# A two-block transformer kernel: first products ahead of a modulation step, and modulation columns summed off TensorE

## The chip, the cores and the metric

The kernel runs on one NeuronCore of a Trainium2 chip. Its time is the device time of one execution in microseconds (us). The engines are TensorE (PE, matrix products), VectorE (DVE), ScalarE (ACT), GpSimd (POOL) and SyncE (SP), which issues the DMAs. Each engine executes its instructions in the order in which the program issues them, and waits at semaphores for the others.

## The reference, cut to what matters

Two transformer-like blocks follow each other on a sequence of 512 rows and 1024 channels, in fp32. The change lies in the first block only.

```python
mod = split((silu(c) @ ada_w + ada_b), 6)          # six vectors of 1024
h  = modulate(rmsnorm(x,  norm1_g), mod[0], mod[1])  # h*(1+scale)+shift
hc = modulate(rmsnorm(ctx, norm1_g), mod_c[0], mod_c[1])
z  = h @ w_in                 # q, k, v, spatial gate u and v, conv a and gate
kvc = hc @ w_in[:, 512:1536]  # keys and values of the context
att = neighbourhood_attention(q, k, v, kc, vc, na_rpb)
y  = concat(att, spatial_gating(u, v), conformer_conv(a, gate)) @ w_out
x  = x + mod[2] * y
h2 = modulate(rmsnorm(x, norm2_g), mod[3], mod[4])
x  = x + mod[5] * conv_ffn(h2, w_up, conv_w, w_down)
x  = rmsnorm(x, final_norm_g)
# second block: stick-breaking attention, gated convolution, feed-forward (unchanged)
```

The matrix `ada_w` has 1024 rows (8 groups k of 128) and 6144 columns, here counted as 12 chunks of 512. Chunks 0 to 3 are the first shift and scale, for `c` and `c_ctx`; chunks 4 and 5 are mod[2], 6 and 7 are mod[3], 8 and 9 are mod[4], 10 and 11 are mod[5], the gate of the feed-forward.

## The kernel before, in words

Activations lie with channels on the 128 partitions and the 512 rows along the free axis. Every large fp32 product is made of three products of split operands: ACT writes the high part (`whi`, `h_hi`, L201, L167, L170), DVE or POOL subtracts it for the low part (`wlo`, `h_lo`, L209, L168, L171), and PE multiplies hi by hi, lo by hi and hi by lo (L160 to L162).

Weights come in units of 1 MB through SP's queue into three raw buffers. `ws.need(u)` makes the split of the units up to two ahead and issues the next load as soon as a raw buffer is free, which is when DVE has made its `wlo`. SP's queue holds at most eight transfers that have not landed.

The stages around the change, in order:

1. *Start.* PE multiplies junk (L487, L489) while inputs come. `first_rows(k)` sums the chunks 0 to 3 of step k as four column strips of a 128x256 tile, ACT copies the sum to `arow`, `first_mod(k)` (L530, its products L533) brings it into columns, `first_h(k)` makes the modulated `h[k]` and `first_split(k)` the split weights.
2. *First loop*, k = 0 to 7: `first_mm` (L562) multiplies 6 column tiles that accumulate over k; rows and modulation of step k+2 lie between its two halves. From k = 3 on `ada_fetch` (DMA L573) loads four 256 KB tiles of `ada_w` a call.
3. *Input projection*, weight unit by weight unit: p_u(0), p_u(1), p_q[0](0), p_q[0](1), p_q[1](0), p_q[1](1), each a tile of 24 products of 512 columns. Behind each of them stands an `ada_tick`. Then come v tiles 0 to 3, with a tick behind 1 and 3, the context's v tiles, the second half of v with two `gating` calls between, and the k projection with the attention.
4. *Modulation.* A round is four chunks over the eight k. `ada_step` multiplies the four tiles of one k (L481) into four strips of one PSUM tile; behind the last k ACT copies the tile to `arow` (L584). A tick first runs `ada_end` if a round is complete: four products (L591) bring the row into columns and DVE adds the bias (L594). Then it does two steps and fetches two. Round 0 is the chunks 4, 5, 8, 9 and round 1 the chunks 6, 7, 10, 11; the `ada_end` of round 1 stands behind tile 1 of the second v loop (L873).
5. *Work of the other engines there.* DVE makes 60 conv taps (L697, L699) that are dealt out between its other instructions at a rate per tile. `make_hc` (from L757) makes the context's `hc`: DVE `cs` (L761), ACT `hc` (L765), DVE the low part (L767), for three, two and three k: behind p_q[0](1), p_q[1](0) and p_q[1](1). ACT takes the spatial gate's weights `sgw` (L733, `sg_hi`) and the transposed `vgt` (L751) behind p_q[0](0).
6. *Feed-forward.* For each of 22 column tiles two up products; `evac_up` (L1224) makes the convolution and the gated product on ACT, DVE and POOL. The down projection adds `mod[40:48]` times its product to x.

What sets the order is the code itself: it issues each engine's instructions in a fixed order, `tick` deals out the taps, and the tiles' buffers come from pools of 80 slots and 8 PSUM banks.

Of the kernel before, what the change touches and what calls it, by code (L numbers as in the profile page):

```python
# [9 lines left out]
F32 = mybir.dt.float32  # L10
F32R = mybir.dt.float32r
AF = mybir.ActivationFunctionType
ALU = mybir.AluOpType
AX = mybir.AxisListType

P = 128
T = 512
D = 1024
KD = D // P
# [112 lines left out]
def program(ctx: ExitStack, tc: tile.TileContext, A, outT):  # L132
    nc = tc.nc
    V, S, G, PE = nc.vector, nc.scalar, nc.gpsimd, nc.tensor

    def pool(name, bufs, space=None, stack=ctx):
        kw = {"space": space} if space else {"reuse_waits": "tile"}
        return stack.enter_context(tc.tile_pool(name=name, bufs=bufs, **kw))

    ps = pool("ps", 8, bass.MemoryType.PSUM)  # L140
    cp = pool("const", 1)
# [5 lines left out]
    def bank(name="bank", cols=T):  # L147
        return ps.tile([P, cols], F32, tag="b", name=name, padded_shape=[P, T])

    def slot(dt=F32, name="slot", cols=T):  # L150
        t = sl.tile([P, T], dt, tag="s", name=name)
        return t if cols == T else t[:, :cols]
# [11 lines left out]
    def split(hi, lo, src, scale=None, eng=None):  # L164

        if scale is None:
            S.activation(hi, src, AF.Copy)  # L167
            (eng or V).tensor_sub(lo, src, hi)  # L168
        else:
            S.activation(hi, src, AF.Copy, scale=scale)  # L170
            V.scalar_tensor_tensor(lo, src, scale, hi, op0=ALU.mult, op1=ALU.subtract)  # L171
# [87 lines left out]
    def tile_gen(pj, m, acts, b, ts=slice(0, T), ks=None):  # L259

        for n, k in enumerate(ks or range(pj.nk)):
            mm3(b[:, ts], pj.part(m, k), [a[:, ts] for a in acts[k]], n == 0, n == pj.nk - 1)
            yield 3

    def tiles(pj, ms, acts, evac):

        for m in ms:
            b = bank()
            yield from tile_gen(pj, m, acts, b)

            ws.hi(ws.early(pj.at[m, pj.nk - 1][0] + 1))
            evac(m, b)
            ws.lo()
            tick()

    def run(gen):
        for _ in gen:
            pass
# [163 lines left out]
    for k in range(KD):  # L442
        t = slot(name="xs")
# [8 lines left out]
    def pc(name, i, n=1):  # L452
        a = PCOL[name][0]
        return par[:, a + i : a + i + n]

    ones = cp.tile([P, 1], F32, name="ones")
    G.memset(ones, 1.0)
    ident = cp.tile([P, P], F32, name="ident")
# [8 lines left out]
    sc = cp.tile([P, KD, 32], F32, name="sc")  # L467
# [2 lines left out]

    sel = cp.tile([P, 2], F32, name="sel")
    V.tensor_reduce(out=sel, in_=ident.rearrange("p (g j) -> p j g", g=4)[:, 0:2, :], op=ALU.add, axis=AX.X)
    pick = ident.rearrange("p (g j) -> p g j", g=4)[:, :, 0]

    mod = cp.tile([P, 48], F32, name="mod")
# [3 lines left out]
    def ada_matmul(out, g, kk, rhs, start, stop):  # L479

        PE.matmul(out[32 * g : 32 * g + 32, : rhs.shape[1]], sc[:, kk, :], rhs, start=start, stop=stop,  # L481
                  tile_position=(0, 32 * g), skip_group_check=True)
# [5 lines left out]
    def idle(k, n=T):  # L488
        PE.matmul(junk[:, :n], ident, xs[k][:, :n], start=True, stop=True)  # L489
# [40 lines left out]
    def first_mod(k):  # L530
        b, r = fb.pop(k)
        for t in range(2):
            PE.matmul(b[:, 256 + 2 * t : 258 + 2 * t], r[:, t * P : (t + 1) * P], sel, start=True, stop=True)  # L533
        a = PCOL["ada_b"][0] + k
        ab = par[:, a : a + KD + 1 : KD].unsqueeze(2).to_broadcast([P, 2, 2])
        V.tensor_add(mod2[:, k], b[:, 256:260].rearrange("p (t v) -> p t v", t=2), ab)
        V.scalar_tensor_tensor(gs[:, k, :], mod2[:, k, 1, :], 1.0, pc("norm1_g", k).to_broadcast([P, 2]),
                               op0=ALU.add, op1=ALU.mult)

    def first_split(k):  # L540
        wr = fw[k]
        hi = whi_p.tile([P, 1024], F32R, tag="whi", name="whi")[:, : NF * P]
        lo = wlo_p.tile([P, 1024], F32R, tag="wlo", name="wlo")[:, : NF * P]
        S.activation(hi, wr, AF.Copy)
        V.tensor_sub(lo, wr, hi)
        fw[k] = hi, lo

    def first_h(k, between=None):
        h[k] = pair("h")
        s_ = mod2[:, k, 0, 0:1]  # L550
        V.scalar_tensor_tensor(xs[k], xs[k], gs[:, k, 0:1], rxs, op0=ALU.mult, op1=ALU.mult)
        S.activation(h[k][0], xs[k], AF.Identity, bias=s_)
        if between:
            between()
        V.scalar_tensor_tensor(h[k][1], xs[k], s_, h[k][0], op0=ALU.add, op1=ALU.subtract)

    def first_mm(k, ms):
        hi, lo = fw[k]

        for w_, a, s0, s1 in ((hi, 0, True, False), (lo, 0, False, False), (hi, 1, False, True)):  # L560
            for m in ms:
                PE.matmul(first[m], w_[:, m * P : (m + 1) * P], h[k][a], start=s0 and k == 0, stop=s1 and k == KD - 1)  # L562


    ROUNDS = (4, 5, 8, 9), (6, 7, 10, 11)
    ada_live, ada_todo, ada_bank = [], [(r, kk) for r in range(2) for kk in range(KD)], {}

    def ada_fetch():
        if ada_todo:
            r, kk = ada_todo.pop(0)  # L570
            raw = [slot(name="ada") for _ in range(4)]
            for t, c in zip(raw, ROUNDS[r]):
                nc.sync.dma_start(t, A["ada_w"][kk * P : (kk + 1) * P, c * T : (c + 1) * T])  # L573
            ada_live.append((r, kk, raw))

    def ada_step():
        r, kk, raw = ada_live.pop(0)
        if kk == 0:
            ada_bank[r] = bank("adab")
        for g in range(4):  # L580
            ada_matmul(ada_bank[r], g, kk, raw[g], kk == 0, kk == KD - 1)
        if kk == KD - 1:
            t = slot(name="arow")
            S.activation(t, ada_bank[r], AF.Copy)  # L584
            ada_ends.append((r, t))

    def ada_end():
        r, t = ada_ends.pop(0)
        b = ada_bank.pop(r)
        for q in range(4):  # L590
            PE.matmul(b[:, 4 * q : 4 * q + 4], t[:, q * P : (q + 1) * P], pick, start=True, stop=True)  # L591
        for g in (0, 2):
            j = 4 * ROUNDS[r][g]
            V.tensor_add(mod[:, j : j + 8].rearrange("p (g q) -> p g q", q=4),  # L594
                         b[:, :16].rearrange("p (q g) -> p g q", g=4)[:, g : g + 2],
                         pc("ada_b", j, 8).rearrange("p (g q) -> p g q", q=4))

    ada_ends = []

    def ada_tick(n=2):  # L600

        if ada_ends:
            ada_end()
        for _ in range(min(n, len(ada_live))):
            ada_step()
            ada_fetch()
# [14 lines left out]
    rxs = slot(name="rxs")  # L621
    S.activation(rxs, rxb, AF.Copy)
    first_rows(1)
    idle(1)
    del junk
    first_mod(1)
    first_h(1)
    first_split(1)
    first += [bank(f"first{m}") for m in range(NF)]
    for k in range(KD):  # L630
        if k + 3 < KD:
            first_ada(k + 3)
            first_w(k + 3)
        elif k == 5:
            ws.load(0)
        if k >= 3:
            ada_fetch()
        first_mm(k, range(3))
        if k + 2 < KD:
            first_rows(k + 2)  # L640
            first_split(k + 2)
        first_mm(k, range(3, NF))
        if k + 2 < KD:
            first_mod(k + 2)
            first_h(k + 2)
        del fw[k]
    wr_.clear()
    ws.need(0)
    cs = []
    for q in range(4):  # L650
        t = slot(name="cs")
# [66 lines left out]
    first_out()  # L718
    conv_taps()
    lv.rate = LR[0]  # L720
    run(tiles(p_u, (0,), h, evac_u))
    ada_tick()
    cacc = slot(name="cacc", cols=CTX)
    S.activation(cacc, cs[0], AF.Square)
    for k in range(1, KD):
# [20 lines left out]
    for i in range(4):  # L746
        b = bank("vgT", cols=256)
# [31 lines left out]
    for i in range(4):  # L779
# [3 lines left out]
        t = slot(F32R, "vn")  # L783
# [83 lines left out]
    for i in range(4):  # L867
        if i == 3:
            take(kg, KD + 1)
        v_tile(p_v[1], 1, h, i, vt[i])  # L870
        if i in (0, 2):
            gating(i // 2)
        if i == 1:  # L873
            ada_end()
    for i in range(3):
        for q in range(2):
            G.tensor_scalar(vs[i][q][0:64, :], vt[i][q][64:128, :], 1.0, 0.0, op0=ALU.mult, op1=ALU.add)
# [15 lines left out]
    def place(n):  # L893

        return n // 8, n % 4, n // 4 % 2
# [139 lines left out]
    for n in range(NA + OUT + 2):  # L1035
        if n < NA:
            hp, blk, j = place(n)
            if n in QD:
                i = 1 + QD.index(n)
# [37 lines left out]
        for i, steps in PLAN.get(n, ()):  # L1077
            if len(begun) == i:
                b = bank()
# [144 lines left out]
    def evac_up(i, b):  # L1224
        t = gate.pop(i)
        S.activation(t, t, AF.Silu)
        V.tensor_mul(t, t, b)  # L1227
        act[i] = pair("act")
        split(*act[i], t, eng=G)

    def between():
        V.scalar_tensor_tensor(gs2, mod[:, 32:40], 1.0, pc("norm2_g", 0, 8), op0=ALU.add, op1=ALU.mult)
# [40 lines left out]
    g = values()  # L1273
# [142 lines left out]
    for n in range(32 + O2 + 2):  # L1416
# [17 lines left out]
        q = n - O2  # L1434
# [111 lines left out]
    out = outT.rearrange("(k p) n -> p k n", p=P)  # L1546
# [47 lines left out]
    g = half_gen(1)  # L1594
    take(g, 6)
    r = half_root(0)
# [10 lines left out]
    for j in range(4):  # L1607
# [4 lines left out]
        else:  # L1612
            t = bank("fr").rearrange("p (k n) -> p k n", k=2)
# [21 lines left out]
```

## Time and profile before

| what | value |
|---|---|
| time, median of 3 runs | 1387.94 us (1387.94 to 1388.05) |
| profiled execution, its own time | 1387.97 us |
| its span | 1386.1 us |
| mean granted clock of TensorE | 0.997 |
| busy: PE, DVE, ACT, POOL | 99%, 57%, 40%, 17% |
| DMA read, written | 147.67 MB, 2.10 MB |

The span runs from the first to the last instruction; the execution's own time lies around it. Busy PE is the time in which at least one product is under way. The ends of products are modelled, so a product's time is best read from the start of the next one: 24 products of 512 columns are 72 split products. A record on PE is a pass: an fp32 product shows as two.

### The profile page before, as it was taken

The numbers are of one execution on the slowest core, as the hardware profiler recorded it, in microseconds if no ns is written. First come the engines' busy times: TensorE is split into PE (matmuls) and PEld (weight loads), VectorE is DVE, ScalarE is ACT, GpSimd is POOL, SyncE is SP. The second block draws the span as 40 slices with busy tenths as digits, with TensorE's granted clock in tenths as the row PEclk, the third lists the DMA queues.
The fourth block names the chain that finished last, engine by engine and source line by source line (L and its number), as shares of the span: only waits on it lengthen the run. The fifth ranks groups of instructions, "written<-read, shape, count | busy, mean of one in ns | idle before, by whom it ended". The sixth has DMA issues, their size and how long they took to land.

```text
span 1386.1 us, 18751 instructions
## 1 busy us (share of the span) xinstructions
PE 1369.9 (99%) x7468; PEld 1151.0 (83%) x7468; DVE 783.8 (57%) x1158; ACT 559.4 (40%) x901; POOL 238.8 (17%) x254
## 2 busy tenths in 40 slices
PE   9999999999999999999999999999999999999997
PEld 5768999898888888888888888888897888888887
DVE  4579688465444443434458964635378866663223
ACT  4433258445333333323345543323455534343231
POOL 0022324101111110112034431000231111110100
PEclk9999999999999999999999999999999999999998
DMA  9992452323232222322373122233211332222221
GB/s 362 376 350 92 121 136 66 125 89 108 77 120 92 91 99 76 107 84 91 91 199 112 41 92 91 91 110 104 92 62 65 122 113 97 91 84 84 84 84 61
DMA packets 140887, 160.41 MB, mean 116 GB/s; under 512 B 5633, under 2 KB 117505, under 8 KB 140801
## 3 DMA queue, kind: packets, MB, share of 16 engines
q1 hardware_dynamic: 139360, 156.91, 34.4%
q10 hardware_dynamic: 1440, 2.31, 0.5%
q8 instruction: 58, 0.95, 0.3%
q14 instruction: 29, 0.23, 0.1%
HBM read 147.67 MB, written 2.10 MB: 108 GB/s over the span
## 4 chain that ended last, share of the span: by engine, by line
PE 91%; DVE 4%; ACT 1%; issue 1%; POOL 1%; DMA 0%; POOLq 0%; SPq 0%; DVEq 0%; ACTq 0%
PE bank L160 24%; PE bank L162 24%; PE bank L161 24%; PE first L562 3%; PE v L160 1%; PE v L162 1%; PE v L161 1%; PE adab L481 1%; PE s L904 1%; PE pt L932 1%; DVE wlo L209 1%; PE f L160 1%; PE o L160 1%; PE o L161 1%; PE o L162 1%
## 5 line engine op out<-in xcount | busy, mean ns | idle before, releaser
L209 DVE TENSOR_TENSOR wlo<-wraw,whi 128x1024 fp32r<-128x1024 f32 (+1 forms) x211 | 275.7, 1314 | 106.6 <-ACT whi L201 106.4
L162 PE MATMUL bank<-h_hi,wlo 128*128 128x512 f32 (+1 forms) x816 | 304.2, 373 | 1.7 <-DVE wlo L209 1.7
L161 PE MATMUL bank<-h_lo,whi 128*128 128x512 f32 (+1 forms) x816 | 305.5, 374 | 0.2
L160 PE MATMUL bank<-h_hi,whi 128*128 128x512 f32 (+1 forms) x816 | 304.9, 374 | 0.0
L201 ACT ACTIVATE whi<-wraw 128x1024 fp32r<-128x1024 f32 (+1 forms) x211 | 217.3, 1036 | 102.4 <-PE bank L161 89.5
L160 PEld LDWEIGHTS bank<-h_hi,whi 128*128 128x128 f32 x816 | 153.6, 188 | 30.1 <-PE adab L481 1.7
L162 PEld LDWEIGHTS bank<-h_hi,wlo 128*128 128x128 f32 x816 | 153.5, 188 | 29.6 <-DVE wlo L209 2.5
L161 PEld LDWEIGHTS bank<-h_lo,whi 128*128 128x128 f32 x816 | 153.5, 188 | 28.2 <-DVE h_lo L1501 0.3
L168 POOL TENSOR_TENSOR act_lo<-cv,act_hi 128x512 fp32r<-128x512 f32 x44 | 61.2, 1392 | 429.0 <-ACT act_hi L167 429.0
L160 PE MATMUL bank<-act_hi,whi 128*128 128x512 f32 x308 | 119.8, 389 | 0.0
L161 PE MATMUL bank<-act_lo,whi 128*128 128x512 f32 x308 | 119.8, 389 | 0.0
L162 PE MATMUL bank<-act_hi,wlo 128*128 128x512 f32 x308 | 119.8, 389 | 0.0
L160 PE MATMUL bank<-hb_hi,whi 128*128 128x512 f32 x288 | 116.0, 403 | 1.5 <-DVE wt_lo L1397 1.5
L162 PE MATMUL bank<-hb_hi,wlo 128*128 128x512 f32 x288 | 112.5, 391 | 0.0
L161 PE MATMUL bank<-hb_lo,whi 128*128 128x512 f32 x288 | 112.4, 390 | 0.0
L167 ACT ACTIVATE act_hi<-cv 128x512 fp32r<-128x512 f32 x44 | 27.8, 633 | 129.3 <-DVE cv L1227 73.0
L161 PEld LDWEIGHTS bank<-act_lo,whi 128*128 128x128 f32 x308 | 57.8, 188 | 12.1
L162 PEld LDWEIGHTS bank<-act_hi,wlo 128*128 128x128 f32 x308 | 57.8, 188 | 12.0
L160 PEld LDWEIGHTS bank<-act_hi,whi 128*128 128x128 f32 x308 | 57.8, 188 | 11.9
L160 PEld LDWEIGHTS bank<-hb_hi,whi 128*128 128x128 f32 x288 | 54.1, 188 | 11.5 <-DVE wt_lo L1397 1.7
L162 PEld LDWEIGHTS bank<-hb_hi,wlo 128*128 128x128 f32 x288 | 54.1, 188 | 11.5
L161 PEld LDWEIGHTS bank<-hb_lo,whi 128*128 128x128 f32 x288 | 54.2, 188 | 9.0
(386 smaller groups left out, 2425.7 us busy)
## 6 DMA issues: line engine op xcount, KB each, us to landing
wraw<-in_w_in SPq DMA_DIRECT2D x23, 1024.0 KB, 5.4
wraw<-in_ffn_w_up SPq DMA_DIRECT2D x22, 1024.0 KB, 4.9
wraw<-in_w_up SPq DMA_DIRECT2D x22, 1024.0 KB, 4.9
ada<-in_ada_w SPq DMA_DIRECT2D x64, 256.0 KB, 5.5
ada<-in_ada_first SPq DMA_DIRECT2D x32, 256.0 KB, 5.8
wraw<-in_w_out SPq DMA_DIRECT2D x8, 1024.0 KB, 4.8
wraw<-in_ffn_w_down SPq DMA_DIRECT2D x8, 1024.0 KB, 5.0
wraw<-in_w_down SPq DMA_DIRECT2D x8, 1024.0 KB, 5.1
```

The costliest lines, as they stand in the source:

```text
L160: PE.matmul(out, lhs[0], rhs[0], start=start, stop=False, **kw)
L161: PE.matmul(out, lhs[0], rhs[1], start=False, stop=False, **kw)
L162: PE.matmul(out, lhs[1], rhs[0], start=False, stop=stop, **kw)
L167: S.activation(hi, src, AF.Copy)
L168: (eng or V).tensor_sub(lo, src, hi)
L201: S.activation(h, src, AF.Copy)
L209: V.tensor_sub(l, src, h)
L481: PE.matmul(out[32 * g : 32 * g + 32, : rhs.shape[1]], sc[:, kk, :], rhs, start=start, stop=stop, tile_position=(0, 32 * g), skip_group_ch ...
L562: PE.matmul(first[m], w_[:, m * P : (m + 1) * P], h[k][a], start=s0 and k == 0, stop=s1 and k == KD - 1)
L904: PE.matmul(st_s[n][:, ks], qp[hp][a][j][:, qs], k_, start=a == 0, stop=a == 1)
L932: PE.transpose(pt[:, c * P : (c + 1) * P], e[:, c * P : (c + 1) * P], ident)
```

## The change

It does four things.

1. The junk product `idle(1)` goes, and modulation, h and weight split of step 1 stand behind the first three column tiles of step 0.
2. Round 0: the steps k = 0, 1, 2 are not multiplied on PE. `ada_sum` in the first loop (k = 4, 5, 6) forms the sum over k for each of 128 partitions: four DVE products, four DVE multiply-adds, then four ACT products and four POOL additions. Four products with `one0` add the sum to the PSUM tile behind the last step.
3. Round 1 holds only chunks 6 and 7, two k per step, so four steps. The tick behind p_u(0) becomes three fetches ahead of it. The `ada_end` of round 1 has no place of its own any more: the next tick runs it.
4. Chunks 10 and 11 are fetched in the first eight up tiles of the feed-forward, two tiles at a time, summed over k on DVE in the next, and brought into columns by eight products of one column in tile 10.

```diff
+    ROUNDS = ([[(k, c) for c in (4, 5, 8, 9)] for k in range(KD)],
+              [[(2 * k + i, c) for i in range(2) for c in (6, 7)] for k in range(KD // 2)])
+    NV = 3
+    def ada_sum():
+        r, kk, raw = ada_live.pop(0)
+        for g in range(4):
+            if kk == 0:
+                ada_acc.append(slot(name="adaacc"))
+                V.tensor_scalar(ada_acc[g], raw[g], sc[:, kk, 0:1], 0.0, op0=ALU.mult, op1=ALU.add)
+            elif kk == NV - 1:
+                S.activation(raw[g], raw[g], AF.Copy, scale=sc[:, kk, 0:1])
+                G.tensor_add(ada_acc[g], ada_acc[g], raw[g])
+            else:
+                V.scalar_tensor_tensor(ada_acc[g], raw[g], sc[:, kk, 0:1], ada_acc[g], op0=ALU.mult, op1=ALU.add)
...
     def ada_step():
         r, kk, raw = ada_live.pop(0)
-        if kk == 0:
+        first_ = NV if r == 0 else 0
+        if kk == first_:
             ada_bank[r] = bank("adab")
         for g in range(4):
-            ada_matmul(ada_bank[r], g, kk, raw[g], kk == 0, kk == KD - 1)
-        if kk == KD - 1:
+            ada_matmul(ada_bank[r], g, ROUNDS[r][kk][g][0], raw[g], kk == first_, r == 1 and kk == KD // 2 - 1)
+        if r == 0 and kk == KD - 1:
+            for g in range(4):
+                PE.matmul(ada_bank[r][32 * g : 32 * g + 32, :], one0, ada_acc[g], start=False, stop=True,
+                          tile_position=(0, 32 * g), skip_group_check=True)
+        if kk == len(ROUNDS[r]) - 1:
             t = slot(name="arow")
             S.activation(t, ada_bank[r], AF.Copy)
...
+    def gate_fetch(k):
+        gate_raw.append([slot(name="ada") for _ in range(2)])
+        for i, t in enumerate(gate_raw[-1]):
+            ada_load(t, k, 10 + i)
+    def gate_step(k):
+        for i, t in enumerate(gate_raw.pop(0)):
+            if k == 0:
+                gate_acc.append(slot(name="gacc"))
+                V.tensor_scalar(gate_acc[i], t, sc[:, k, 0:1], 0.0, op0=ALU.mult, op1=ALU.add)
+            else:
+                V.scalar_tensor_tensor(gate_acc[i], t, sc[:, k, 0:1], gate_acc[i], op0=ALU.mult, op1=ALU.add)
+    def gate_end():
+        b = bank("gsum", cols=8)
+        for j in range(8):
+            PE.matmul(b[:, j : j + 1], gate_acc[j // 4][:, j % 4 * P : j % 4 * P + P], ones, start=True, stop=True)
+        V.tensor_add(mod[:, 40:48], b, pc("ada_b", 40, 8))
...
     first_rows(1)
-    idle(1)
     del junk
-    first_mod(1)
-    first_h(1)
-    first_split(1)
...
         first_mm(k, range(3))
+        if k == 0:
+            first_mod(1)
+            first_h(1)
+            first_split(1)
...
             first_h(k + 2)
+        if k in (4, 5, 6):
+            ada_sum()
...
+    for _ in range(3):
+        ada_fetch()
     run(tiles(p_u, (0,), h, evac_u))
-    ada_tick()
...
         if i in (0, 2):
             gating(i // 2)
-        if i == 1:
-            ada_end()
...
+        if 1 <= i < KD + 1:
+            gate_step(i - 1)
+        if i < KD:
+            gate_fetch(i)
+        if i == KD + 2:
+            gate_end()
```

What stands in PE's row of instructions behind v tile 1, in the kernel before (each row is one form, with the number of times that it stands there in a row; the last products of v tile 1 and the first of v tile 2 frame it):

```order
L161 MATMUL v<-wlo,h_hi 128x256
L162 MATMUL v<-whi,h_lo 128x256
L481 MATMUL adab<-ada,sc 32x512 x8
L160 MATMUL v<-whi,h_hi 128x256
L161 MATMUL v<-wlo,h_hi 128x256
```

The same place in the changed kernel:

```order
L161 MATMUL v<-wlo,h_hi 128x256
L162 MATMUL v<-whi,h_lo 128x256
L624 MATMUL adab<-pick_112,arow 128x2 x4
L160 MATMUL v<-whi,h_hi 128x256
L161 MATMUL v<-wlo,h_hi 128x256
```

The two steps of round 1 are gone from here, and its `ada_end`, which reads `arow`, stands in their place.

On ACT, from the last weight split and q tile to the copy `arow` of round 1, in the kernel before (`hc` is the context stream of the last `make_hc`, `v_hi` and `vn` are the high parts of the v tiles and of the normalised gate rows):

```order
L170 ACTIVATE q_hi<-bank 128x512
L765 ACTIVATE hc<-cs,mod_113 128x256 x3
L201 ACTIVATE whi<-wraw 128x1024
L167 ACTIVATE v_hi<-v 128x256
L167 ACTIVATE vn<-vgt 128x256
L167 ACTIVATE v_hi<-v 128x256
L167 ACTIVATE vn<-vgt 128x256
L167 ACTIVATE v_hi<-v 128x256
L167 ACTIVATE vn<-vgt 128x256
L167 ACTIVATE v_hi<-v 128x256
L167 ACTIVATE vn<-vgt 128x256
L584 ACTIVATE arow<-adab 128x512
```

The same place in the changed kernel:

```order
L170 ACTIVATE q_hi<-bank 128x512
L823 ACTIVATE hc<-cs,mod_115 128x256 x3
L615 ACTIVATE arow<-adab 128x512
L201 ACTIVATE whi<-wraw 128x1024
L167 ACTIVATE v_hi<-v 128x256
L167 ACTIVATE vn<-vgt 128x256
```

The copy has moved ahead of the four v tiles, and now stands directly behind the last three `hc`.

On SP, from the weight loads at the end of the first loop to the load of `sgw`, in the kernel before (`cs` is the context, `rows` are rows of the spatial gate):

```order
L185 DMA wraw<-in_w_in 128x8x256 x3
L652 DMA cs<-in_ctxT 128x2x256 x4
L573 DMA ada<-in_ada_w 128x512 x8
L185 DMA wraw<-in_w_in 128x8x256
L573 DMA ada<-in_ada_w 128x512 x8
L731 DMA rows<-in_rows 128x512
L732 DMA rows<-in_rows 128x256
L733 DMA sgw<-in_sg_wT 128x512
```

The same place in the changed kernel:

```order
L185 DMA wraw<-in_w_in 128x8x256 x3
L709 DMA cs<-in_ctxT 128x2x256 x4
L592 DMA ada<-in_ada_w 128x512 x12
L185 DMA wraw<-in_w_in 128x8x256
L592 DMA ada<-in_ada_w 128x512 x8
L789 DMA rows<-in_rows 128x512
L790 DMA rows<-in_rows 128x256
L791 DMA sgw<-in_sg_wT 128x512
```

Twelve modulation tiles instead of eight stand ahead of the next weight load, so four more ahead of `sgw`.

## Rows read from the trace of the kernel before

**Rows 1.** The page: busy us by engine, and the chain's shares by engine.

```profile
PE 1369.9 (99%) x7468; PEld 1151.0 (83%) x7468; DVE 783.8 (57%) x1158; ACT 559.4 (40%) x901; POOL 238.8 (17%) x254
...
PE 91%; DVE 4%; ACT 1%; issue 1%; POOL 1%; DMA 0%; POOLq 0%; SPq 0%; DVEq 0%; ACTq 0%
```

**Rows 2.** Windows: length, busy of PE, PEld, DVE, ACT, POOL, clock, DMA share, GB/s.

```profile
60.00:80.00 20.00, 20.00 (x103) 13.71 (x102) 12.48 (x13) 10.64 (x19) 7.61 (x7) 1.00 1.04 378
...
100.00:120.00 20.00, 20.00 (x146) 14.44 (x139) 18.77 (x31) 5.38 (x11) 9.38 (x12) 1.00 0.44 158
...
1378.00:1380.00 2.00, 0.31 (x3) 0.12 (x2) 1.65 (x3) 0.00 (x0) 0.82 (x1) 0.75 0.00 0
```

**Rows 3.** Timeline of PE: start, us, line, operation, tiles, records, idle before.

```profile
82.18 0.50 PE L391 MATMUL sums<-ones,cacc 128*128 128x1 f32 x4
...
115.04 1.92 PE L481 MATMUL adab<-ada,sc 128*32 128x512 f32 x16
116.90 0.39 PE L160 MATMUL v<-whi,h_hi 128*128 128x256 f32 x1
...
134.74 0.28 PE L162 MATMUL mix<-sg_hi,vn 128*128 128x256 f32 x1
...
137.74 0.95 PE L591 MATMUL adab<-ident,arow 128*128 128x4 f32 x8
138.55 0.36 PE L160 MATMUL v<-whi,h_hi 128*128 128x256 f32 x1
...
142.95 0.40 PE L160 MATMUL k<-h_hi,whi 128*128 128x512 f32 x1
```

**Rows 4.** Timeline of ACT, 84 to 126 us.

```profile
84.40 0.61 ACT L167 ACTIVATE sg_hi<-sgw 128x512 fp32r<-128x512 f32 x1
...
86.03 1.07 ACT L201 ACTIVATE whi<-wraw 128x1024 fp32r<-128x1024 f32 x1
91.07 0.60 ACT L170 ACTIVATE q_hi<-bank 128x512 fp32r<-128x512 f32 x1 [3.97 <-PE bank L162]
...
119.49 1.31 ACT L765 ACTIVATE hc<-cs,mod 128x256 fp32r<-128x256 f32 x3 [6.06 <-DVE cs L761]
...
124.90 0.60 ACT L584 ACTIVATE arow<-adab 128x512 f32<-128x512 f32 x1 [0.85 <-PE adab L481]
```

**Rows 5.** Timeline of DVE, 56 to 132 us.

```profile
56.40 2.36 DVE L209 TENSOR_TENSOR wlo<-wraw,whi 128x1024 fp32r<-128x1024 f32 x2 [0.20 <-ACT whi L201]
...
91.70 0.69 DVE L171 SCALAR_TENSOR_TENSOR q_lo<-bank,q_hi 128x512 fp32r<-128x512 f32 x1 [0.38 <-ACT q_hi L170]
...
105.54 4.63 DVE L699 SCALAR_TENSOR_TENSOR cacc<-ag,par,cacc 128x510 f32<-128x510 f32 x4
...
118.97 1.27 DVE L761 SCALAR_TENSOR_TENSOR cs<-cs,gs,rcbs 128x256 f32<-128x256 f32 x3
...
131.40 0.42 DVE L168 TENSOR_TENSOR vn<-vgt,vn 128x256 fp32r<-128x256 f32 x1
```

**Rows 6.** Timelines of ACT and PE at the start.

```profile
16.49 0.72 ACT L552 ACTIVATE h_hi<-xs,mod 128x512 fp32r<-128x512 f32 x1 [1.86 <-DVE xs L551]
...
18.02 0.61 PE L533 MATMUL ada<-sel,arow 128*128 128x2 f32 x4
18.49 0.94 PE L562 MATMUL first<-h_hi,whi 128*128 128x512 f32 x3
```

**Rows 7.** Timeline of SP's DMA issues: the load of sgw.

```profile
77.54 0.33 SPq L733 DMA_DIRECT2D sgw<-in_sg_wT  x1
```

**Rows 8.** DMA issues, 50 to 100 us: count, KB each, median us to landing.

```profile
sgw<-in_sg_wT SPq DMA_DIRECT2D x1, 256.0 KB, 4.8
```

**Rows 9.** PE's groups by form, 4.5 to 6.8 and 7.5 to 11 us: busy, mean ns.

```profile
L489 PE MATMUL junk<-xs,ident 128*128 128x512 f32 x2 | 1.9, 1061 | 0.0
...
L489 PE MATMUL junk<-xs,ident 128*128 128x512 f32 x7 | 3.4, 607 | 0.1
```

**Rows 10.** Timeline of DVE in the up tiles of the feed-forward.

```profile
410.88 0.75 DVE L1220 SCALAR_TENSOR_TENSOR cv<-bank,par,cv 128x511 f32<-128x511 f32 x1 [2.14 <-ACT cv L1218]
```

More of the change, by code (lines that the diff above doesn't have):

```diff
@@ L472, in program @@
     V.tensor_reduce(out=sel, in_=ident.rearrange("p (g j) -> p j g", g=4)[:, 0:2, :], op=ALU.add, axis=AX.X)
+    pick2 = cp.tile([P, 2], F32, name="pick2")
+    V.tensor_reduce(out=pick2, in_=ident.rearrange("p (i c j) -> p c i j", i=2, c=2)[:, :, :, 0], op=ALU.add, axis=AX.X)
     pick = ident.rearrange("p (g j) -> p g j", g=4)[:, :, 0]
@@ L562, in first_mm, with ada_load @@
                 PE.matmul(first[m], w_[:, m * P : (m + 1) * P], h[k][a], start=s0 and k == 0, stop=s1 and k == KD - 1)
-    ROUNDS = (4, 5, 8, 9), (6, 7, 10, 11)
-    ada_live, ada_todo, ada_bank = [], [(r, kk) for r in range(2) for kk in range(KD)], {}
+    ROUNDS = ([[(k, c) for c in (4, 5, 8, 9)] for k in range(KD)],
+              [[(2 * k + i, c) for i in range(2) for c in (6, 7)] for k in range(KD // 2)])
+    NV = 3
+    ada_acc = []
+    one0 = cp.tile([P, 32], F32, name="one0")
+    G.memset(one0, 0.0)
+    G.memset(one0[:, 0:1], 1.0)
+    def ada_sum():
[9 more added lines that the diff above has]
+                V.scalar_tensor_tensor(ada_acc[g], raw[g], sc[:, kk, 0:1], ada_acc[g], op0=ALU.mult, op1=ALU.add)
+    ada_live, ada_todo, ada_bank = [], [(r, kk) for r in range(2) for kk in range(len(ROUNDS[r]))], {}
+    def ada_load(t, k, c):
+        nc.sync.dma_start(t, A["ada_w"][k * P : (k + 1) * P, c * T : (c + 1) * T])
     def ada_fetch():
@@ L571, in ada_fetch @@
             raw = [slot(name="ada") for _ in range(4)]
-            for t, c in zip(raw, ROUNDS[r]):
-                nc.sync.dma_start(t, A["ada_w"][kk * P : (kk + 1) * P, c * T : (c + 1) * T])
+            for t, (k, c) in zip(raw, ROUNDS[r][kk]):
+                ada_load(t, k, c)
             ada_live.append((r, kk, raw))
@@ L589, in ada_end @@
         b = ada_bank.pop(r)
+        w_ = pick if r == 0 else pick2
+        n = w_.shape[1]
         for q in range(4):
-            PE.matmul(b[:, 4 * q : 4 * q + 4], t[:, q * P : (q + 1) * P], pick, start=True, stop=True)
-        for g in (0, 2):
-            j = 4 * ROUNDS[r][g]
+            PE.matmul(b[:, n * q : n * q + n], t[:, q * P : (q + 1) * P], w_, start=True, stop=True)
+        for g, j in ((0, 16), (2, 32)) if r == 0 else ((0, 24),):
             V.tensor_add(mod[:, j : j + 8].rearrange("p (g q) -> p g q", q=4),
-                         b[:, :16].rearrange("p (q g) -> p g q", g=4)[:, g : g + 2],
+                         b[:, : 4 * n].rearrange("p (q g) -> p g q", g=n)[:, g : g + 2],
                          pc("ada_b", j, 8).rearrange("p (g q) -> p g q", q=4))
+    gate_raw, gate_acc = [], []
+    def gate_fetch(k):
[14 more added lines that the diff above has]
+        V.tensor_add(mod[:, 40:48], b, pc("ada_b", 40, 8))
+        gate_acc.clear()
     ada_ends = []
```

## Prediction

> **What bounds the kernel now.** I read the page's busy times first, then its chain, then the stretches from 60 to 160 us engine by engine. TensorE (PE) is busy for 99% of the span and makes 91% of the chain that ended last [rows 1]. So PE work that disappears is time gained, unless PE comes to wait for something else. VectorE (DVE) is at 57% over the whole span, but that mean hides one stretch: from 100 to 120 us DVE is busy for 18.77 of 20 us [rows 2], and there its work, the conv taps and the context stream hc, runs behind PE. In the kernel before nobody on PE waits for the end of that backlog before the k projection. The reader is to hold on to this: PE is full everywhere, but from 83 to 148 us DVE and the ScalarE (ACT) work behind it are the late ones.
>
> **The change part by part.** The sum is made against the profiled execution, 1387.97 us (span 1386.1 and 1.87 around it), which is 0.03 above the median of 1387.94.
>
> *PE work removed.* A modulation tick of two steps is 16 records, from 115.04 to 116.90: 1.86 us; one step is 0.93 [rows 3]. An ada_end runs from 137.74 to 138.55: 0.81. In program order: the tick behind p_u(0) goes (−1.86, and about 0.2 for two changes of matmul shape: −2.06); the tick behind p_q[0](1) gains four one0 products, priced as a step (+0.93); the tick behind p_q[1](1) loses a step (−0.93); the tick behind v tile 1 becomes an ada_end (−1.86 + 0.81 = −1.05); the tick behind v tile 3 goes (−1.86); the ada_end in the p_v[1] loop goes (−0.81). Sum −5.8.
>
> *The place that decides: the ada_end that now stands between v tiles 1 and 2.* Its first product needs the copy arow of round 1. In the kernel before the copy is made at 124.90 [rows 4] and first read at 137.74 [rows 3], 12 us later. In the changed program the copy is issued on ACT behind the three hc of the last make_hc, and these wait for DVE's cs products. In the trace those cs start at 118.97 [rows 5], the first hc at 119.49 after ACT has been idle for 6.06 us waiting for them, and the three hc take 1.31 [rows 4]. With a copy of 0.60 the arow is there at 119.49 + 1.31 + 0.60 = 121.40, less S, by which DVE's chain moves forward. PE arrives far earlier: v tile 1 ends at 115.04, and what is removed ahead of it (0.8 at the start, below, 2.06, and +0.93 − 0.93) brings it there at 112.2. PE executes in order, so v tile 2 and all behind it wait 121.40 − 112.2 − S = 9.2 − S. Everything that was gained ahead of it is given back: from there on only the time of the copy counts.
>
> *How large S is.* DVE's chain from 83 us on starts with PE's q tiles, so at best S = 2.06 + 0.8 = 2.86. What may hold it: DVE's q_lo at 91.70 stood only 0.38 idle, behind ACT's q_hi at 91.07 [rows 4, 5], and ACT reaches q_hi through sg_hi, which waits for the transfer sgw. *The start*, for the 0.8: the first product follows h_hi(0), which ends at 17.21, instead of starting at 18.49, 1.28 earlier; the modulation pair that moves behind it costs its 0.47 (18.02 to 18.49) there: 0.8 [rows 6]. sgw is issued at 77.54 [rows 7] and lands 4.8 us later [rows 8], at 82.34; ACT took it at 84.40. Two things make it later. Four more ada transfers stand ahead of it on SP's queue: at 378 GB/s of a full DMA (share 1.04 [rows 2]) 262,144 bytes take 0.69 us, so 2.8. And the third weight load is issued when DVE has made the wlo of 56.40 to 58.76 [rows 5]; directly ahead of these now stand four scalar_tensor_tensor of ada_sum, 0.75 each by the row of that form [rows 10], 3.0 in all, of which the 0.8 of the start and the 0.2 idle there cover 1.0: +2.0. sgw lands at 87.1, and from sg_hi to the end of whi ACT takes 2.7 (84.40 to 87.10 [rows 4]): q_hi at 89.8, S = 1.3. The ends: no delay at the load leaves S at 2.86, since q_hi then waits for PE alone at 88.2; and if ada_sum's four POOL adds stretch the wlo beside them as POOL stretched the taps at 105.54 (four in 4.63, 1.16 each against 0.75 [rows 5, 10]), the two wlo take 1.3 more and S is 0.0. I take 1.3, worked out from the nearest rows. The Trainium skill ("GPSIMD Engine Reference", 8. Key points) says that GpSimd shares its SBUF interfaces with VectorE and collides with DVE instructions of two SBUF inputs; the 1.16 agrees, and by that rule alone S would be the 0.0.
>
> *From the copy to the k projection.* In the trace 27.91 us pass from 115.04 to 142.95 [rows 3]; of these 1.86, 1.86 and 0.81 go and 0.81 for the moved ada_end come in: 24.2. So k starts at 121.40 − 1.3 + 24.2 = 144.3 against 142.95: +1.35. Nothing between waits longer than that: DVE and ACT work of the v tiles moves with PE's stall.
>
> *The clock.* With S = 1.3 PE stands still for 7.9 us. The trace shows both levels: the first junk matmuls of 128x512 take 1061 ns a record and the later ones 607 [rows 9], so PE, which began at 1.46, ran at the 1.2 GHz level until about 6.8; and at the end, when PE's work runs out (busy 0.31 in 1378 to 1380), the granted clock of that slice is 0.75, a fall from 1.00 to 0.50 in the middle of it [rows 2]. Nowhere in the trace does PE pause for 8 us and go on. If it falls here, the nearest row for the price is the start: 5.3 us at the lower level, in which 1 − 607/1061 = 43% is lost: 2.3 us. Bounds 0 (no fall) and 2.7 (half of 5.3). I take 2.3, since the end shows a fall sooner than 8 us after the last long group. The Trainium skill ("TensorE: Matmul & The Clock Gate", Part 1) says the same from the other side: the throttled 1.2 GHz is the default, and only activity lifts it. By this rule the loss comes; without a fall the sum is 2.3 less.
>
> *The feed-forward gate.* gate_end adds 8 products of one column, 16 records. By L391 (four in 0.50 [rows 3]) they are 2.0, by the ada_end (eight in 0.81) 1.6; I take 1.8, on PE between two up tiles and covered by nothing: +1.8. The 16 DVE products (two per up tile, 0.75 each, 1.5) fall into DVE's waits for PE, 2.14 idle in the tightest of the rows that I read there [rows 10]; the 16 transfers stand behind a weight load each. Cost nothing, and 12 us if that cover were gone.
>
> *Sum.* +1.35 (all before k) + 2.3 (clock) + 1.8 (gate) = +5.4: 1387.97 + 5.4 = 1393.4. From the bounds: S 2.86 and no fall give −0.2 + 0 + 1.6 = +1.4 (1389.4); S 0.0, 2.7 and 2.0 give +2.65 + 4.7 = +7.4 (1395.3).
>
> **The rivals.** (a) *PE waits, but the clock stays.* For it: no row shows a pause of this length inside the work, so the fall is not proven. Against: the fall at the end. Time: 1393.4 − 2.3 = 1391.1.
> (b) *The copy is in time and the change pays, faster than before.* One point decides: the arow copy ends by 112.2, so S would have to be 9.2. For it: the taps that fill DVE are not urgent, and ACT is idle for 6.06 there. Against: DVE's own order puts cs behind them, and its 18.77 of 20 us. Then PE keeps −5.8 − 0.8; next late is vn, whose last low half ends at 131.82 [rows 5] and is read at 134.74 [rows 3], 2.9 later; PE would come there 2.86 + 1.05 + 1.86 = 5.8 earlier and DVE 1.3, so it waits 1.6. Sum −6.6 + 1.6 + 1.8 = −3.2: 1384.8.
> (c) *The gate's DVE work is not hidden.* For it: each up tile already has DVE's two conv products, a product and the weight split. Against: 2.14 of idle for 1.5. In full 12 us: 1405. It decides if DVE has no idle left in up tiles 1 to 8.
>
> **How the numbers follow.** This kernel's measurement can tell 0.2%, 2.8 us, from no change: 1385.2 to 1390.7. Forecast, with a fall: 0.60; (a) 0.18; (b) 0.13; (c) 0.09. The forecast case spans 1391.5 to 1395.3; (a) 1389.4 to 1393, half of it within the bound; (b) lies faster but for a little; (c) slower. Faster 0.12, same 0.12, slower 0.76. The range takes in the forecast, (a) and the lower part of (c), and leaves (b) and a full (c) out: 1388.5 to 1396.5.
>
> **What would show it.** Right: on PE an idle time of 6 to 9 us ahead of the pick2 products, released by ACT's arow; hc's ACT idle before them, released by DVE's cs; sgw landing about 5 us later than before and q_hi released by ACT, not by PE; a granted clock of 0.50 for some us behind the stall; k at 143 to 146; gsum 1.6 to 2.0 with no new DVE wait of PE in the up tiles. Wrong: no idle at the pick2 products (then b), a clock of 1.00 throughout (a), or up tiles longer than before (c). The step I am least sure of is S, the one that I am surest of the order on ACT.

## The result and the profile after

The changed kernel takes 1400.0 us (1399.47 to 1400.54, 4 runs) against 1387.99 for the kernel before: ratio on record 1.0083, interval 1.0071 to 1.0096 (not quite the quotient of the two medians). It is 12.0 us slower; the forecast was 5.4 slower, with a range that ended at 1396.5. The profiled execution is 1399.72, its span 1398.0 against 1386.1, so 11.9 of the difference lie in the span.

Where PE waited, in the changed kernel (us in total, times, longest):

```profile
PE adab L624 <- ACT arow L615: 10.9, 1, 10.9
PE bank L162 <- DVE wlo L209: 2.7, 4, 1.0
PE bank L160 <- DVE wt_lo L1459: 1.5, 1, 1.5
...
PE bank L160 <- ACT vgt L809: 0.6, 1, 0.6
```

In the kernel before the first and the last of these do not exist, and the second is shorter:

```profile
PE bank L162 <- DVE wlo L209: 1.7, 3, 0.8
```

So there is one large new wait, and it stands between v tiles 1 and 2. The timeline of PE there, and at the start of the k projection, answers to [rows 3]:

```profile
113.94 0.28 PE L162 MATMUL v<-whi,h_lo 128*128 128x256 f32 x1
125.14 1.87 PE L624 MATMUL adab<-pick,arow 128*128 128x2 f32 x8 [10.92 <-ACT arow L615]
126.87 0.56 PE L160 MATMUL v<-whi,h_hi 128*128 128x256 f32 x1
...
151.90 0.40 PE L160 MATMUL k<-h_hi,whi 128*128 128x512 f32 x1
```

PE came at 114.2 and went on at 125.1. The ada_end took 1.73 us to the next start, where one of its length took 0.81 before, and k starts at 151.90 instead of 142.95. What PE waited for, on ACT (answers to [rows 4]):

```profile
92.28 0.63 ACT L167 ACTIVATE sg_hi<-sgw 128x512 fp32r<-128x512 f32 x1 [9.39 <-DMA sgw<-in_sg_wT]
...
94.82 0.62 ACT L170 ACTIVATE q_hi<-bank 128x512 fp32r<-128x512 f32 x1
...
123.30 1.30 ACT L823 ACTIVATE hc<-cs,mod 128x256 fp32r<-128x256 f32 x3 [6.06 <-DVE cs L819]
124.51 0.57 ACT L615 ACTIVATE arow<-adab 128x512 f32<-128x512 f32 x1
```

ACT stood 9.39 us idle for sgw; q_hi came at 94.82 instead of 91.07, and everything that DVE does behind q_lo came as much later: hc at 123.30 instead of 119.49. Read upwards, DVE and POOL show why sgw was late (answers to [rows 5]):

```profile
55.31 4.82 DVE L587 SCALAR_TENSOR_TENSOR adaacc<-ada,sc,adaacc 128x512 f32<-128x512 f32 x4
60.05 5.67 DVE L209 TENSOR_TENSOR wlo<-wraw,whi 128x1024 fp32r<-128x1024 f32 x3
...
95.46 0.69 DVE L171 SCALAR_TENSOR_TENSOR q_lo<-bank,q_hi 128x512 fp32r<-128x512 f32 x1 [6.87 <-ACT q_hi L170]
```

```profile
56.21 7.29 POOL L585 TENSOR_TENSOR adaacc<-adaacc,ada 128x512 f32<-128x512 f32 x4 [54.34 <-DVE adaacc L587]
```

```profile
52.75 12.24 SPq L185 DMA_DIRECT2D wraw<-in_w_in  x3
...
87.21 0.33 SPq L791 DMA_DIRECT2D sgw<-in_sg_wT  x1
```

A merged row hides how long each instruction took. The view of the tiles `adaacc` and `wlo` gives the shortest, the median and the longest in ns:

```profile
L587 DVE SCALAR_TENSOR_TENSOR adaacc<-ada,sc,adaacc x4: 745/1264/1786, 55.3 to 58.3; 128x512 f32<-128x512 f32 x4
L209 DVE TENSOR_TENSOR wlo<-wraw,whi x3: 1212/2305/2311, 60.1 to 64.5; 128x1024 fp32r<-128x1024 f32 x3
```

POOL's four additions run from 56.21 to 63.50. The two multiply-adds that began before them took 0.745 us each, the two beside them 1.79; the first two low parts, beside them, took 2.31, and the third, begun at 64.50, 1.21. The second low part ends at 64.59 and the third weight load is issued at 64.62. In the kernel before the row of these loads is:

```profile
51.28 7.87 SPq L185 DMA_DIRECT2D wraw<-in_w_in  x3
```

It ends at 59.15, the one of the changed kernel at 64.99: the third load is issued 5.84 later, and sgw 9.7 later than in [rows 7].

The clock, in windows across the pause:

```profile
116.00:118.00 2.00, 0.00 (x0) 0.00 (x0) 1.21 (x5) 1.25 (x2) 0.00 (x0) 0.89 0.00 0
118.00:120.00 2.00, 0.00 (x0) 0.00 (x0) 1.97 (x3) 0.00 (x0) 0.00 (x0) 0.50 0.00 0
...
128.00:130.00 2.00, 2.00 (x11) 2.00 (x10) 1.96 (x5) 0.00 (x0) 0.00 (x0) 0.50 0.78 236
130.00:132.00 2.00, 2.00 (x14) 2.00 (x14) 1.52 (x4) 0.06 (x1) 0.00 (x0) 0.69 0.82 289
132.00:134.00 2.00, 2.00 (x19) 2.00 (x18) 1.64 (x4) 0.63 (x2) 0.00 (x0) 1.00 0.01 4
```

It falls to the 1.2 GHz level while PE stands still, stays there through the first 6 us of new work, and is back behind 131 us.

### The profile page after: what moved, and what is told of

Read it like the earlier page. It is cut to its first block, busy times and chain, and to the rows that moved or that the text cites. A ratio compares the mean times of both kernels' runs of the same rounds, so it can differ in the third digit from the quotient of the medians.

```text
span 1398.0 us, 18714 instructions
## 1 busy us (share of the span) xinstructions
PE 1368.3 (98%) x7434; PEld 1154.4 (83%) x7434; DVE 807.5 (58%) x1183; ACT 561.8 (40%) x905; POOL 247.0 (18%) x260
## 3 DMA queue, kind: packets, MB, share of 16 engines
q10 hardware_dynamic: 1440, 2.31, 0.5%
## 4 chain that ended last, share of the span: by engine, by line
PE 87%; DVE 6%; DMA 2%; ACT 2%; issue 1%; POOL 1%; POOLq 0%; ACTq 0%; DVEq 0%
PE bank L162 23%; PE bank L160 23%; PE bank L161 23%; PE first L564 2%; DVE wlo L209 1%; PE v L160 1%; PE v L161 1%; PE v L162 1%; PE s L960 1%; DMA ada<-in_ada_w 1%; PE pt L988 1%; DMA ada<-in_ada_first 1%; PE o L160 1%; PE o L161 1%; PE o L162 1%
## 5 line engine op out<-in xcount | busy, mean ns | idle before, releaser
L209 DVE TENSOR_TENSOR wlo<-wraw,whi 128x1024 fp32r<-128x1024 f32 (+1 forms) x211 | 284.0, 1355 | 104.8 <-ACT whi L201 104.6
L1586 DVE TENSOR_TENSOR y<-bank,R 128x512 f32<-128x512 f32 x44 | 30.3, 689 | 54.3 <-PE bank L162 52.2
```

Of the source, the lines that this page charges most:

```text
L209: V.tensor_sub(l, src, h)
L1586: V.tensor_mul(y, b, R3)
```

## The experiments

All ratios are set against runs of the kernel before on the same chip (1388.1 to 1388.5 in the three groups); where a time is compared with the changed kernel, it is with its 1400.0 above.

**e1, the ada_end where it was.** Tests whether the wait for the copy is the loss.

```diff
         split(*vn[i], vt_[i])
-        if i % 2:
-            ada_tick()
...
             gating(i // 2)
+        if i == 1:
+            ada_end()
```

> The changed kernel with one edit: round 1's ada_end stands where the kernel before had it, behind tile 1 of the second v loop. Theory (PE waits 10.9 us for the copy arow at v tile 2): that wait goes; the DVE chain is still as late as measured (q_hi at 94.8 instead of 91.1), so PE next waits for vn at the gating products: its last low half comes 11.1 us behind the whi of the chain (as before), at about 136.1, PE would be there at 130.1. k at about 144.3 instead of 151.9, and 1391.5 to 1394 in all, the upper end if the clock falls in this shorter wait too. Rival (the copy is only the place where a general lateness shows, or the time is lost in the feed-forward): 1399 or more.

Measured: 1393.5 (ratio 1.0039, 1.0024 to 1.0054), 6.5 better than the changed kernel. The chain is as late as before the edit (sg_hi at 92.72, copy ended at 125.6), and PE now waits in other places:

```profile
PE mix L162 <- DVE vn L168: 3.1, 2, 2.2
...
PE v L160 <- ACT hc L823: 2.1, 1, 2.1
```

As the theory said, in the upper part of its range; the clock fell here as well (0.73 in 135 to 140 us). The rival is out. But the edit gives back 6.5 of the 12 us: the chain is still late, and PE meets it at the next products that need it. What is new is the 2.1 for hc, which I had not counted.

**e2, two sums instead of three, none on POOL.** Tests what makes the load late.

```diff
-    NV = 3
+    NV = 2
...
-            elif kk == NV - 1:
-                S.activation(raw[g], raw[g], AF.Copy, scale=sc[:, kk, 0:1])
-                G.tensor_add(ada_acc[g], ada_acc[g], raw[g])
...
-        if k in (4, 5, 6):
+        if k in (5, 6):
             ada_sum()
```

> The changed kernel with two modulation steps instead of three summed off PE (k = 0 and 1, on DVE alone, in loop steps 5 and 6); the third is a PE step again (+0.93), ACT's scaling and POOL's additions are gone. Theory (POOL's additions beside DVE stretch ada_sum and the weight low parts, and so hold the third weight load and sgw): four multiply-adds 3.0 us instead of 4.82, three wlo 3.5 instead of 5.67, the load issued at about 60.7 instead of 64.6, sgw landed at about 88 instead of 92.3, the arow there at about 121 instead of 125.1; 1395.5 to 1397. Rival (sgw is late because of the transfers ahead of it, POOL does not matter): the load at 64 or later, 1400 to 1401.

Measured: 1397.24 (1.0066, 1.0049 to 1.0083), 0.24 above the range of the theory. The timeline of DVE, its instructions one by one (ns), and SP's issues of the loads and of sgw:

```profile
55.52 1.67 DVE L582 TENSOR_SCALAR adaacc<-ada,sc 128x512 f32<-128x512 f32 x4
57.10 2.73 DVE L584 SCALAR_TENSOR_TENSOR adaacc<-ada,sc,adaacc 128x512 f32<-128x512 f32 x4
59.75 3.49 DVE L209 TENSOR_TENSOR wlo<-wraw,whi 128x1024 fp32r<-128x1024 f32 x3
```

```profile
L584 DVE SCALAR_TENSOR_TENSOR adaacc<-ada,sc,adaacc x4: 742/743/744, 57.1 to 59.1; 128x512 f32<-128x512 f32 x4
L209 DVE TENSOR_TENSOR wlo<-wraw,whi x3: 1214/1215/1216, 59.8 to 62.0; 128x1024 fp32r<-128x1024 f32 x3
```

```profile
52.53 9.97 SPq L185 DMA_DIRECT2D wraw<-in_w_in  x3
...
83.59 0.33 SPq L788 DMA_DIRECT2D sgw<-in_sg_wT  x1
```

The same instructions at the same place take 0.74 and 1.22 us without POOL beside them, and 1.79 and 2.31 with it. The edit also takes ACT's scaling out, but that is not the cause: in the changed kernel ACT's scaling runs from 54.51 to 57.06, and the two multiply-adds that began beside it and ahead of POOL took 0.745. The last load is issued 2.5 us earlier (62.1) and sgw 3.6 earlier, though more DVE work stands in a row here (both sums, from 55.52 on, which is why the load comes later than the 60.7 expected). POOL's share in the lateness is shown. It is not all of it: sgw is still issued 6.05 later than in the kernel before (83.59 against 77.54), and the load is 3.35 of that (62.50 against 59.15). PE's wait for the copy fell only from 10.9 to 9.6.

**e4, sgw loaded first.** Tests the link from sgw to the copy.

```diff
+    nc.sync.dma_start(rows[0], A["rows"][:, :512])
+    nc.sync.dma_start(rows[1], A["rows"][:, 512:])
+    nc.sync.dma_start(sgw, A["sg_wT"])
     for _ in range(3):
         ada_fetch()
...
     ada_tick()
-    nc.sync.dma_start(rows[0], A["rows"][:, :512])
-    nc.sync.dma_start(rows[1], A["rows"][:, 512:])
-    nc.sync.dma_start(sgw, A["sg_wT"])
```

> The changed kernel with the loads of rows and sgw issued ahead of the twelve modulation tiles instead of behind twenty and a weight load. Theory (ACT's wait for sgw holds q_hi and with it DVE's chain up to hc and the copy): sgw landed before 75, ACT has no wait for it, q_hi released by PE at about 89.3 instead of 94.8, arow there at about 119.6 instead of 125.1, PE's wait about 6 instead of 10.9: 5.5 us faster, 1394.5, the clock's loss about as it is. Rival (the chain is late for DVE's own work, whatever sgw does): arow at 124 or later, 1399 to 1400.

Measured: 1394.92 (1.0049, 1.0034 to 1.0064). ACT's timeline:

```profile
83.15 0.61 ACT L167 ACTIVATE sg_hi<-sgw 128x512 fp32r<-128x512 f32 x1
...
89.84 0.60 ACT L170 ACTIVATE q_hi<-bank 128x512 fp32r<-128x512 f32 x1 [3.99 <-PE bank L162]
...
119.53 0.57 ACT L615 ACTIVATE arow<-adab 128x512 f32<-128x512 f32 x1
```

No wait for sgw; q_hi is released by PE; the copy is 5.0 us earlier, PE's wait 6.3 instead of 10.9. The link is shown. It also tries the forecast's other terms: here S is 1.3 (121.40 against the copy's end at 120.10), the value that I had taken, and the time is 1394.9 where I had 1393.4. That the value is the same is luck: the forecast reached 1.3 through a late sgw, and here sgw holds nothing. With PE alone ahead of it q_hi starts at 89.84, not at the forecast's 88.2, so 1.3 is what was left of the bound of 2.86.

**e3 and e9, PE kept at work in the pause.** They test the clock's term. 40 products of 128 columns (e3), or 48 of 512 (e9, whose edit is shown), stand ahead of the ada_end; nothing reads them.

```diff
+        if i == 1:
+            fill = bank("fill")
+            for _ in range(48):
+                PE.matmul(fill, h[0][0][:, :P], h[0][0], start=True, stop=True)
         if i % 2:
             ada_tick()
```

> The changed kernel with 40 products of the identity with itself on PE ahead of round 1's ada_end, whose result nothing reads: about 9.6 us of work in the time in which PE waits for the copy. Theory (the pause lowers the clock, and its return costs time): granted clock 1.00 from 112 to 136, ada_end in 0.9 instead of 1.73 and v tiles 2 and 3 in 5.8 instead of 7.75: 2.9 us faster than the changed kernel, 1397. Rival (the clock costs nothing that counts, because other work is late there anyway): 1400.

> The changed kernel with 48 products of 512 columns in place of the 40 of 128 columns ahead of round 1's ada_end (result read by nothing): 48 times 0.227 is 10.9 us, all of PE's wait. With the 40 small ones the clock still fell for a while behind them (0.82 and 0.84 in 125 to 135 us) and v tiles 2 and 3 took 7.3 us. Theory (the loss is the clock's fall, and it goes when PE's work does not thin out): clock 1.00 from 110 to 140, v tiles 2 and 3 in 5.8 us, k 2.9 us earlier than in the changed kernel, 1397.1. Rival (the v tiles are slow behind the wait for another reason): 7 us or more for them at a clock of 1.00, and 1398 or more.

Measured: e3 1397.81 (1.0071, 1.0056 to 1.0086) and e9 1398.32 (1.0068, 1.0052 to 1.0083). Windows of e3, then of e9:

```profile
126.00:128.00 2.00, 2.00 (x18) 2.00 (x19) 1.21 (x2) 1.91 (x5) 0.00 (x0) 1.00 0.00 0
128.00:130.00 2.00, 2.00 (x12) 2.00 (x12) 1.96 (x5) 0.00 (x0) 0.00 (x0) 0.55 0.41 83
130.00:132.00 2.00, 2.00 (x13) 2.00 (x12) 1.96 (x5) 0.69 (x2) 0.00 (x0) 0.60 1.09 384
```

```profile
126.00:128.00 2.00, 2.00 (x18) 2.00 (x19) 1.21 (x2) 1.92 (x5) 0.00 (x0) 1.00 0.00 0
128.00:130.00 2.00, 2.00 (x19) 2.00 (x19) 1.96 (x5) 0.06 (x1) 0.00 (x0) 1.00 0.37 89
130.00:132.00 2.00, 2.00 (x19) 2.00 (x18) 1.97 (x5) 0.63 (x2) 0.00 (x0) 1.00 1.08 380
```

In e3 PE still waits 2.0 us behind the small products, and the clock falls for some 4 us when the v tiles are already running. In e9 there is no pause and no fall, v tiles 2 and 3 take 5.8 us instead of 7.75, and k starts at 149.9 instead of 151.9. The stretch agrees with the theory. Neither median reaches its expectation (1397 and 1397.1). For e9 the profiled execution, the slowest of its four, shows a part of why: a wait of 1.3 us in the second block (PE for a transfer of k_hi, ahead of the product that starts at 706.61 in the kernel before) that the other traces do not have. The two medians do not tell e3 from e9. That the fall costs 2 to 3 us rests on the stretch.

**e5 and e6, one part alone.** The gate's part without sums of round 0, with the old start and the late ada_end (e5); the new start alone in the kernel before (e6; its edit is the first part of the change).

```diff
 # e5, against the changed kernel, besides e1's edit and the old start
-    NV = 3
+    NV = 0
...
-        if k in (4, 5, 6):
-            ada_sum()
...
-    for _ in range(3):
-        ada_fetch()
     run(tiles(p_u, (0,), h, evac_u))
+    ada_tick()
```

> The kernel before with one part of the change alone: the feed-forward gate's columns summed on DVE in the up tiles, so that round 1 has four steps instead of eight; no sums of round 0 off PE, the old start, round 1's ada_end where it was. Theory (the gate costs its 1.85 us of PE and nothing else, and takes two ticks of 1.86 off the v tiles): -3.7 on PE, +1.85, and about 1 us of wait for vn at the gating products, to which PE comes 3.7 us earlier: 1386.5 to 1388, no change that a run can tell. Rival (the 16 DVE products or the 16 transfers hold the up tiles): 1390 or more.

> The kernel before with the new start alone: no junk product after the second modulation row, modulation, h and weight split of step 1 behind the first products. Theory (all of PE and with it DVE's chain move 0.87 us forward, as at 20.8 us of the changed kernel's trace): 1387.1. Rival (given back before the k projection, since DVE's chain does not follow): 1388.0.

Measured: e5 1388.64 (1.0003, 0.9994 to 1.0012), above its theory's range, and e6 1387.54 (0.9994, 0.9985 to 1.0003). In e5 PE comes earlier by two ticks and then waits 1.6 us for vn; the gate's products take 1.8. What is left, about 0.4, the runs cannot tell from nothing; half a microsecond of the profiled execution is lost at the start, in unchanged code. No up tile waits: the rival is out. In e6 the shift of −0.92 at 24.3 us stays to the end of the trace (−0.87 at the last products); the median is 0.66 lower, which the interval does not tell from zero.

**e7, e8, e10, e11, versions put together.** All have the new start and the edits of e1 and e4. e11 is that and no more, with the three sums of the change; e7 has e5's edit (no sums off PE); e8 has e2's edit, two sums on DVE, but in loop steps 4 and 5; e10 is e8 with the gating calls one tile later:

```diff
 # e8 and e10, besides the edits of e1, e2 and e4
-        if k in (5, 6):
+        if k in (4, 5):
             ada_sum()
...
 # e10
-        if i in (0, 2):
+        if i in (1, 3):
             gating(i // 2)
```

> A version put together from what the runs showed: the new start, round 1 halved and the gate in the feed-forward, round 1's ada_end late as in the kernel before, sgw loaded ahead of p_u(0), and no sums off PE in the first loop. Theory: -0.87 at the start, -3.7 of ticks, +1.85 gate, +1.3 wait for vn at the gating products: 1386.6; no wait for arow, clock 1.00 from 100 to 150 us. Rival (something of the change that is still in it costs on its own): 1388 or more.

> The same with two steps of round 0 summed on DVE (k = 0 and 1, in loop steps 4 and 5, so none directly ahead of the weight low parts, none on POOL), and three fetches in place of the tick behind p_u(0). Theory (a step off PE is worth its 0.93 where neither POOL nor the queue holds the weights and sgw): PE steps 11 instead of 16, -4.65, -0.87 at the start, +1.85 gate, +0.4 wait for vn: 1384.8. Rival (any DVE sum in the first loop holds the third weight load and so the chain behind it): 1387 or more, with a wait of PE for vn of over 3 us.

> The changed kernel as it is, its third sum on ACT and POOL included, with the two orders mended: round 1's ada_end late, rows and sgw loaded ahead of p_u(0). Theory (POOL's additions cost PE about 1 us at p_u(0), where it waits for the weight low part, which is what the step off PE gains, 0.93): the same as the version with two sums, 1386. Rival (the third sum pays once sgw does not hang on it): 1385.0. Rival (POOL's additions hold DVE's chain in the v tiles too): 1388 or more.

> The version with two sums on DVE and the late ada_end, with the two gating calls one v tile later (behind tiles 1 and 3 instead of 0 and 2). Theory (the last wait that the change left on PE here is 0.8 us for vn at the first gating): that wait goes, 0.8 us faster, 1385.1. Rival (the gating's DVE work then stands in the way of the k projection's low parts): 1386 or more, with a new wait of PE for k_lo, q_lo or bias.

| version | us | ratio | interval | PE waits for vn |
|---|---|---|---|---|
| e7, no sums | 1387.40 | 0.9993 | 0.9985 to 1.0002 | 1.6 |
| e11, three sums | 1387.13 | 0.9990 | 0.9981 to 0.9999 | 1.6 |
| e8, two sums | 1385.94 | 0.9985 | 0.9976 to 0.9993 | 0.8 |
| e10, two sums, gating later | 1384.93 | 0.9975 | 0.9965 to 0.9986 | 0 |

e7 and e8 are about 1 us above their expectations; 0.3 and 0.4 of that are longer waits for vn, the rest is open. Against e7 the two sums gain 1.5. In e8, other than its expectation says, the second sum still stands directly ahead of the low parts (the multiply-adds run from 55.60 to 58.33, the low parts from 58.25); what is gone is POOL beside them, and a low part takes 1.22. e11 lies between its theory and the third reading: its step less on PE does not pay, since PE waits 1.0 us longer for the low parts at p_u(0) and 0.8 longer for vn. e10 met its theory. It beats both kernels, by 3.6 us in this group and by 15 against the changed one.

## Why the prediction was wrong

The sign and the place were right; the term S failed, and with it the range.

- *The order on PE and ACT, the wait for the copy.* Right: the rows show it as forecast, and e1 removes it.
- *S, predicted 1.3 with ends 0.0 and 2.86; measured −3.7* (121.40 against the copy's end at 125.08). The step that failed is the delay of the third weight load: "+2.0" was 5.84. I priced the multiply-adds at 0.75 from a row in which POOL was idle and the two low parts ahead of the load at no change, and let POOL stretch only the low parts, as the far end of a range. In the trace POOL's additions stand beside two of the multiply-adds and both of these low parts: from the first multiply-add to the low parts 4.74 pass instead of 3.0 (55.31 to 60.05), and the two low parts take 4.54 instead of 2.36 (60.05 to 64.59). The row that showed it (the taps at 105.54, 1.16 each) stood in the forecast; it was used for the low parts alone and not for the value, and its factor of 1.5 was itself too small: 1.79 against 0.74 is 2.4, 2.31 against 1.22 is 1.9. The Trainium skill ("GPSIMD Engine Reference", 8. Key points), which names this collision for DVE instructions with two SBUF inputs, agrees with 1.79 against 0.74 and 2.31 against 1.22 in e2. The rest of sgw's lateness, 4.1 of 9.9 where 2.8 was priced for four transfers, lies behind that load: the next weight load comes 2.0 later still (76.24 against 68.36), from there to sgw 1.8 are added (10.97 us instead of 9.18), and 0.2 in its landing. Why the last stretch is longer I did not settle.
- *PE's arrival*, 112.2: it was 114.2; 1.6 of the difference is PE's own waits, 1.0 for a low part at 62.4 and 0.6 for vgt. The copy came 5.0 later than forecast and PE 2.0, so the wait was 10.9 instead of 7.9. The arrival does not change the time: from there on only the copy counts, as forecast.
- *From the copy to k*: predicted 24.2 and 2.3 for the clock, in the trace 26.8 from 125.08 to 151.90.
- *The clock*: it fell, as forecast. Predicted 2.3, measured 2.8 (0.9 in the ada_end, 1.9 in v tiles 2 and 3 against 5.84 in e9). The Trainium skill's rule ("TensorE: Matmul & The Clock Gate", Part 1), that the throttled clock is the default and activity lifts it, agrees: the granted clock is back at 1.00 only after PE has gone on at 125.14, and in e9, where PE does not stop, it stays at 1.00.
- *The gate*: predicted 1.8, measured 1.7 from its first product to the next tile. The DVE work was hidden, as forecast: PE's waits in the up tiles are those of before.

```profile
429.80 1.84 PE L649 MATMUL gsum<-ones,gacc 128*128 128x1 f32 x16
431.50 0.49 PE L160 MATMUL bank<-h_hi,whi 128*128 128x512 f32 x1
```

- *The start*: predicted 0.8; the first product of p_u(0) starts at 60.81 instead of 61.62, 0.8 earlier, and e6 keeps its gain.
- *Sum*: k is 8.95 late, the gate adds 1.7; 1.25 of the span's 11.9 is left, 0.6 of it behind the last instruction of DVE (4.4 us from its start at 1381.67 to the end of the span before, 5.0 from 1392.98 after), the rest in small steps between. Neither is explained. Against the forecast's 5.45 the span has 6.45 more: 5.0 by S, 0.3 from the copy to k with the clock, these 1.25, and 0.1 less at the gate.

Rivals: (a) is out by the clock's windows and (c) by e5 and PE's waits. (b), the copy in time, did not happen; e1 shows that even without that wait DVE's late chain decides.

## What to carry to other kernels

When work leaves an engine that is full, look at what its next instruction now waits for: a product that read a copy made 12 us earlier came to wait 10.9 us for it when its place moved up to the next tick. A price for an instruction is taken from a row with the same neighbours: the same DVE instruction cost 0.74 us with POOL idle and 1.79 beside its additions, and a mean over a merged row (1.20) showed neither. And work of no urgency that stands in front of a weight's low part is paid at the load queue, and shows up far from there, here behind the load, sgw, q_hi, hc and the copy; two sums on DVE alone gained (e8 against e7), the third, with POOL's additions beside the low parts, did not (e11).

## What the runs showed of the hardware that was not expected

While POOL's additions ran beside DVE's multiply-adds and low parts, the two engines kept step. In narrow windows of the timeline DVE's instructions from 56.64 on begin at 56.64, 58.35 and 60.05 and POOL's at 56.21, 57.83, 59.54 and 61.24, each some 1.7 us behind the one before, where DVE alone took 0.66 from one multiply-add to the next (55.31 to 55.97).

The clock can fall when the engine is already at work again. In e3, behind 40 products of 128 columns and a wait of 2.0 us, the granted clock was still 1.00 in 126 to 128 us and then 0.55 and 0.60 in 128 to 132, with PE full in all three windows; in e9, behind 48 products of 512 columns and no wait, it was 1.00 in all of them. Which of the two differences did it was not tried apart. Products of 128 columns are not needed for it: in e1, which has none of the added ones, PE waited 0.9 and 2.2 us for vn, went on at 136.63, and the granted clock fell behind that:

```profile
136.00:138.00 2.00, 1.36 (x8) 1.37 (x9) 1.97 (x5) 0.00 (x0) 0.00 (x0) 0.82 0.00 0
138.00:140.00 2.00, 2.00 (x11) 2.00 (x11) 1.96 (x4) 0.00 (x0) 0.00 (x0) 0.50 0.00 0
```
